# A transformer block in split float32: activations as the stationary operand, and a DMA that makes every fourth low half

## The chip, the cores and the metric

The kernel runs on one core of a Trainium2 chip. The number that counts is the device time of one execution in microseconds (us). The core's engines work side by side: TensorE (PE in the profile, its weight loads PEld), VectorE (DVE), ScalarE (ACT), GpSimd (POOL), and SyncE (SP), which here only issues transfers. They wait for each other through semaphores; 16 DMA engines carry the transfers.

## The reference

One layer of a speech-encoder block on x of 256 tokens by 2048 channels, all float32 (cut to what matters; the biases, the convolution and the scan are left out):

```python
def rms_norm(x, w):
    return x * lax.rsqrt(jnp.mean(x * x, axis=-1, keepdims=True) + NORM_EPS) * w

def swiglu(h, w_gate, w_up, w_down):            # D_FF = 5504
    return (jax.nn.silu(h @ w_gate) * (h @ w_up)) @ w_down

x = x + 0.5 * swiglu(rms_norm(x, n1), ...)      # first half-step
proj = rms_norm(x, mix_norm) @ w_in             # gdn q k v z a b | att q k v | two gates
o_gdn = gdn_branch(...)                         # gated delta rule, 8 heads of 128, chunks of 64
o_att = chunk_attention_branch(...)             # 8 heads of 128, band of 576 keys
merged = (jax.nn.sigmoid(gate_gdn) * (o_gdn @ w_branch_gdn)
          + jax.nn.sigmoid(gate_att) * (o_att @ w_branch_att))
x = x + merged @ w_out
x = x + 0.5 * swiglu(rms_norm(x, n2), ...)      # second half-step
```

Some 400 MB of weights are read once. Each product has 256 rows.

## The kernel before, in words

**Split operands.** Each float32 operand of a large product is an exact pair of float32r halves, hi + lo, and a product is hi·hi + hi·lo + lo·hi. Activations (`xr`, `hid`, `ob`, `oa`, `mg`) lie with channels on partitions, hi and lo side by side, 2 x 256 columns to a channel tile of 128.

**Pieces of weights.** `plan` lists all weights in the order of use, cut into pieces of at most 1024 columns (128 partitions x 1024, 512 KB). `prepare` takes the next piece: SP loads it to `raw` (L194), ACT casts it to `wh` (L197), DVE writes `wl` = `raw` - `wh` (L198). The pools of `raw`, `wh` and `wl` have four buffers each. `take_weights` hands the oldest piece to a product and first calls `prepare` until four pieces are on their way (AHEAD = 4); so the instructions that prepare a piece are put on their engines' queues about three pieces before PE uses it. Every engine runs its own queue in order. A cast waits until PE has done with the piece that held its `wh` buffer before.

**The large products** (`gemm_steps`, L224): a 128 x 128 weight tile is the stationary operand. One matmul takes `wh` with the 512 columns hi | lo of the activations, a second `wl` with the 256 columns hi. That makes 5536 pairs: 4128 in the two feed-forward steps (`pg`, `pu`, `pd`) and 1408 in the mixing part (`pc`, `pwb`, `pgt`, `pwa`, `pwo`); the last output tile uses another form (43 more matmuls). The result has channels on partitions, as the next product wants it. `gather` (L268, L270) joins the two halves of a result, and the factor of the norm, `rb`, the same on all partitions, is multiplied on afterwards. POOL computes the squares for the norms of the later steps.

**The attention projections and z** (`pav`, `paq`, `pak`, `pz`; `gemm_n_steps`, L258 to L260) already have activations stationary: 128 tokens x 128 channels, and the weights move, 352 or 512 columns at a time, three matmuls to a token tile.

**Order.** The program order is the order of the Python code. In the attention and delta-rule stages `weave` puts the small products of the core computation between the pieces of a large product.

Of the kernel before, what the change touches and what calls it, by code (L numbers as in the profile page):

```python
# [23 lines left out]
H = 8  # L24
# [10 lines left out]
def block_kernel(ctx: ExitStack, tc: tile.TileContext, a: dict, out: bass.AP):  # L35
    """Activations are kept transposed (channels on partitions, tokens free), each float32
    matmul operand as an exact pair of float32r halves hi + lo; a product is hi*hi + hi*lo + lo*hi."""
# [23 lines left out]
    # ---------------------------------------------------------------- residual stream  # L61
# [5 lines left out]
    x_blk = [heap([P, 8, T], F32, f"x{b}") for b in range(2)]  # L67

    def x(k):
        return x_blk[k // 8][:, k % 8, :]  # L70

    def load_x(k, n):
        nc.sync.dma_start(x_blk[k // 8][:, k % 8 : k % 8 + n, :], a["x"][:, k : k + n, :])
# [9 lines left out]
    # ---------------------------------------------------------------- helpers  # L83
    def rsqrt(dst, v, n, nm):
        """dst = v ** -0.5 for a small tile of positive v, with a Newton step."""
        s = tp.tile([P, T], F32, name=f"rs_s{nm}", tag="su", bufs=4)[:, :n]
        r = tp.tile([P, T], F32, name=f"rs_r{nm}", tag="su", bufs=4)[:, :n]
# [5 lines left out]
        nc.vector.tensor_mul(dst, r, s)  # L93

    class Xr:
        """x * norm weight as hi | lo, four channel tiles to a block; sums of squares aside."""

        def __init__(self, nm, wi):
            self.nm, self.wi = nm, wi
            self.blk = []  # L100
            self.acc = sp.tile([P, T], F32, name=f"ssq{nm}", tag="ssq", bufs=1)

        def add(self, k):
            if k % 4 == 0:
                self.blk.append(heap([P, 4, 2, T], F32R, f"xr{self.nm}_{k}"))
            b = self.blk[-1][:, k % 4]
            w = vcol(V_N[self.wi] + k)
            nc.scalar.activation(b[:, 0, :], x(k), AF.Copy, scale=w)
            nc.vector.scalar_tensor_tensor(  # L109
                b[:, 1, :], x(k), w, f32(b[:, 0, :]), op0=ALU.mult, op1=ALU.subtract  # L110
            )

        def square(self, k, act=False):
            if act:
                sq = tp.tile([P, T], F32, name=f"sq{self.nm}_{k}", tag="sq") if k else self.acc
                nc.scalar.activation(sq, x(k), AF.Square)
                if k:
                    nc.vector.tensor_add(self.acc, self.acc, sq)
            elif k == 0:
                nc.gpsimd.tensor_mul(self.acc, x(k), x(k))  # L120
            else:
                sq = tp.tile([P, T], F32, name=f"sq{self.nm}_{k}", tag="sq")
                nc.gpsimd.tensor_mul(sq, x(k), x(k))
                nc.gpsimd.tensor_add(self.acc, self.acc, sq)

        def finish(self):
            """rb: 1 / rms for every token, the same on all partitions."""
            ps = acc_bank(f"nps{self.nm}")
            nc.tensor.matmul(ps[:, 0:T], ones, self.acc, start=True, stop=True)
            v = tp.tile([P, T], F32, name=f"nv{self.nm}", tag="su", bufs=4)  # L130
            nc.vector.tensor_scalar(v, ps[:, 0:T], 1.0 / D, EPS, op0=ALU.mult, op1=ALU.add)
            self.rb = sp.tile([P, T], F32, name=f"rb{self.nm}", tag="rb", bufs=2)
            rsqrt(self.rb, v, T, f"n{self.nm}")

        def by_token(self):
            """rn: the same with tokens on partitions, a column a tile."""
            ps = core_bank(f"nbs{self.nm}")
            self.rn = sp.tile([P, 2], F32, name=f"rn{self.nm}", tag="rn")
            for t in range(2):
                nc.tensor.transpose(ps[:, t * P : (t + 1) * P], self.rb[:, t * P : (t + 1) * P], ident)  # L140
                nc.vector.tensor_copy(self.rn[:, t : t + 1], ps[:, t * P : t * P + 1])
# [4 lines left out]
    # every weight of the block, in the order of use, in pieces of at most 1024 columns  # L146
    def pieces(src, width, per):
        for o in range(0, width, per):
            yield src[:, o : min(o + per, width)]

    def t_pieces(srcs, kt):
        for src in srcs:
            yield from pieces(src, kt * P, 1024)

    def n_pieces(src, n):
        yield from pieces(src, KD * n, 1024 // n * n)

    def plan():
        for f in "12":
            tiles = [a[w + f][c] for c in range(KF) for w in ("wg", "wu")]  # L160
            for o in range(0, KD * P, 512):
                yield from (t[:, o : o + 512] for t in tiles[:4])
            yield from t_pieces(tiles[4:], KD)
            yield from t_pieces((a["wd" + f][d] for d in range(KD)), KF)
            if f == "2":
                return
            c0 = 0
            for n in ZG:
                yield from n_pieces(a["wv"][:, c0 * KD : (c0 + n) * KD], n)
                c0 += n  # L170
            for g in range(4):
                yield from n_pieces(a["wa"][g], 512)
            yield from t_pieces((a["wc"][c] for c in range(24)), KD)
            yield from t_pieces((a["wbr"][KD + d] for d in range(KD)), H)
            yield from t_pieces((a["wgt"][KD + d] for d in range(KD)), KD)
            for g in (4, 5):
                yield from n_pieces(a["wa"][g], 512)
            yield from t_pieces((a["wgt"][d] for d in range(KD)), KD)
            yield from t_pieces((a["wbr"][d] for d in range(KD)), H)
            for o in (0, 1024):  # L180
                yield from (a["wo"][d][:, o : o + 1024] for d in range(2))
            yield from t_pieces((a["wo"][d] for d in range(2, KD)), KD)
# [4 lines left out]
    def prepare():  # L187
        """Load the next piece of weights and split it."""
        i, src = next(weights, (None, None))
        if src is None:  # L190
            return
        n = src.shape[1]
        raw = wp.tile([P, 1024], F32, tag="raw", name=f"raw{i}", bufs=4)
        nc.sync.dma_start(raw[:, :n], src)  # L194
        wh = wp.tile([P, 1024], F32R, tag="wh", name=f"wh{i}")
        wl = wp.tile([P, 1024], F32R, tag="wl", name=f"wl{i}")
        nc.scalar.copy(wh[:, :n], raw[:, :n])  # L197
        nc.vector.tensor_sub(wl[:, :n], raw[:, :n], f32(wh[:, :n]))  # L198
        ready.append((wh, wl, n))

    def take_weights(n):
        for _ in range(AHEAD - len(ready)):
            prepare()
        wh, wl, m = ready.popleft()
        assert m == n
# [6 lines left out]
    def weave(core, fill):  # L212
        """Emit core, and between its steps as many pieces of fill as each step asks for."""
# [4 lines left out]
    def gemm_t(ps, kt, mov, fold=False):  # L218
        run(gemm_steps(ps, kt, mov, 8, fold))

    def gemm_steps(ps, kt, mov, per=8, fold=False):
        """ps[:, 0:256] + ps[:, 256:512] = (weights [kt*128, 128]).T @ activations, channels on partitions
        (all in the first half if fold)."""
        mm = lambda dst, w, m, st, en: nc.tensor.matmul(dst, w, m, start=st, stop=en, skip_group_check=True)  # L224
        for k0 in range(0, kt, per):
            c = min(per, kt - k0)
            wh, wl = take_weights(c * P)
            for j in range(c):
                k = k0 + j
                mv = mov(k)  # L230
                wj = slice(j * P, (j + 1) * P)
                if fold:
                    mm(ps[:, 0:T], wh[:, wj], mv[:, 0, :], k == 0, False)
                    mm(ps[:, 0:T], wh[:, wj], mv[:, 1, :], False, False)
                else:
                    mm(ps, wh[:, wj], mv.rearrange("p a t -> p (a t)"), k == 0, False)
                mm(ps[:, 0:T], wl[:, wj], mv[:, 0, :], False, k == kt - 1)
            if k0 + c < kt:
                yield

    def gemm_n(pss, kt, mov, n):
        run(gemm_n_steps(pss, kt, mov, n))

    def gemm_n_steps(pss, kt, mov, n):
        """pss[t] = activations (tokens of tile t on partitions) @ weights [kt*128, n]."""
        per = 1024 // n
        k = 0
        for o in range(0, kt, per):
            c = min(per, kt - o)
            wh, wl = take_weights(c * n)  # L250
            for j in range(c):
                mv = mov(k)
# [724 lines left out]
```

## Time and profile before

| what | value |
|---|---|
| median of 3 runs | 2174.81 us (2174.78 to 2176.48) |
| profiled execution: span from first to last instruction | 2173.8 us |
| what lies around the span: median less span | 1.0 us |
| instructions | 31985 |
| busy: PE / DVE / ACT / POOL | 2161.7 / 1406.2 / 1088.1 / 91.3 us |
| share of 16 DMA engines taken by the load queue | 56.7%, 403.58 MB |
| granted TensorE clock | 1.000 |

A group row of the profile names the line, the engine, the operation, the result and operand tiles by their names in the code, the shape and the count, then the busy time in us, the mean of one in ns, and the idle time of the engine just before them with what ended it. A matmul row of the timeline gives start and duration; matmuls overlap, so the price of one is the distance between two starts.

### The profile page before, as it was taken

Reading aid. Unit: us, or ns where it says so; the run is one execution under the profiler, and the core shown is the slowest. Engines: PE = TensorE matmul, PEld = TensorE weight load, DVE = VectorE, ACT = ScalarE, POOL = GpSimd, SP = SyncE. Lnnn points to the kernel's source line nnn. Section 1 sums busy time; section 2 is a strip of 40 time slices with the busy share of each in tenths; the row PEclk is TensorE's granted clock in tenths of the full one; section 3 lists DMA queues with packets and bytes.
Section 4 is the critical chain, followed back from the end, with each engine's and each line's share of the span. In section 5 each row is a group of like instructions: output and inputs, shape, how many; then the busy total and the mean of one; then the engine's idle time right before and its main releaser. Section 6 shows DMA issues by size and latency. Waiting matters only on the chain.

```text
span 2173.8 us, 31985 instructions
## 1 busy us (share of the span) xinstructions
PE 2161.7 (99%) x12434; PEld 1897.1 (87%) x12434; DVE 1406.2 (65%) x2034; ACT 1088.1 (50%) x1598; POOL 91.3 (4%) x99
## 2 busy tenths in 40 slices
PE   8999999999999999999999999999999999999999
PEld 7888888888888988888888888888888888888888
DVE  7766666665555554888995658767666666655444
ACT  7544444444444444576654645545444444444343
POOL 0000000000111000210000000220000000000000
PEclk9999999999999999999999999999999999999999
DMA  7555555556566665555454555546555555566664
GB/s 241 197 191 190 189 193 188 190 188 187 182 197 189 184 199 191 190 173 170 167 184 136 165 185 188 187 154 218 193 187 191 190 189 192 190 189 191 202 202 134
DMA packets 118985, 405.62 MB, mean 187 GB/s; under 512 B 13345, under 2 KB 19761, under 8 KB 118577
## 3 DMA queue, kind: packets, MB, share of 16 engines
q1 hardware_dynamic: 118832, 403.58, 56.7%
q8 instruction: 97, 1.59, 0.3%
q14 instruction: 56, 0.45, 0.1%
HBM read 401.43 MB, written 2.11 MB: 186 GB/s over the span
## 4 chain that ended last, share of the span: by engine, by line
PE 94%; DVE 3%; DMA 1%; ACT 1%; issue 1%; SPq 0%; POOL 0%; DVEq 0%; ACTq 0%
PE pd L224 22%; PE pu L224 22%; PE pg L224 21%; PE pgt L224 6%; PE pc L224 5%; PE pwo L224 4%; PE pwa L224 2%; PE pwb L224 2%; DVE wl L198 1%; PE pav L258 1%; PE pav L260 1%; PE pav L259 1%; PE pz L258 1%; PE pz L260 1%; PE pz L259 1%; PE paq L260 1%
## 5 line engine op out<-in xcount | busy, mean ns | idle before, releaser
L198 DVE TENSOR_TENSOR wl<-raw,wh 128x1024 fp32r<-128x1024 f32 (+3 forms) x798 | 938.4, 1180 | 690.7 <-ACT wh L197 689.7
L197 ACT CAST wh<-raw 128x1024 fp32r<-128x1024 f32 (+3 forms) x798 | 800.8, 1005 | 976.2 <-issue 569.7
L224 PE MATMUL pg<-xr,wh 128*128 128x512 f32 x1376 | 483.8, 394 | 6.0 <-DVE xr L109 5.9
L224 PE MATMUL pu<-xr,wh 128*128 128x512 f32 x1376 | 483.3, 393 | 0.0
L224 PE MATMUL pd<-hid,wh 128*128 128x512 f32 (+1 forms) x1419 | 477.7, 386 | 0.0
L224 PE MATMUL pg<-xr,wl 128*128 128x256 f32 x1376 | 384.4, 279 | 1.2 <-DVE wl L198 1.2
L224 PE MATMUL pu<-xr,wl 128*128 128x256 f32 x1376 | 384.0, 279 | 0.5 <-DVE wl L198 0.5
L224 PE MATMUL pd<-hid,wl 128*128 128x256 f32 x1376 | 383.3, 279 | 0.0
L224 PEld LDWEIGHTS pg<-xr,wh 128*128 128x128 f32 x1376 | 258.4, 188 | 65.0 <-ACT wh L197 6.1
L224 PEld LDWEIGHTS pd<-hid,wh 128*128 128x128 f32 x1419 | 263.0, 188 | 56.4
L224 PEld LDWEIGHTS pu<-xr,wh 128*128 128x128 f32 x1376 | 258.3, 188 | 58.5
L224 PEld LDWEIGHTS pg<-xr,wl 128*128 128x128 f32 x1376 | 259.9, 189 | 2.4 <-DVE wl L198 2.2
L224 PEld LDWEIGHTS pu<-xr,wl 128*128 128x128 f32 x1376 | 259.8, 189 | 0.9 <-DVE wl L198 0.8
L224 PEld LDWEIGHTS pd<-hid,wl 128*128 128x128 f32 x1376 | 259.3, 188 | 0.0
L224 PE MATMUL pgt<-xr,wh 128*128 128x512 f32 x512 | 181.2, 398 | 0.0
L224 PE MATMUL pgt<-xr,wl 128*128 128x256 f32 x512 | 143.2, 280 | 0.8 <-DVE wl L198 0.8
L224 PE MATMUL pc<-xr,wh 128*128 128x512 f32 x384 | 136.6, 399 | 0.0
L224 PEld LDWEIGHTS pgt<-xr,wh 128*128 128x128 f32 x512 | 96.1, 188 | 22.6
L224 PE MATMUL pc<-xr,wl 128*128 128x256 f32 x384 | 107.4, 280 | 0.0
L224 PEld LDWEIGHTS pgt<-xr,wl 128*128 128x128 f32 x512 | 96.5, 189 | 1.2 <-DVE wl L198 1.2
L224 PE MATMUL pwo<-mg,wh 128*128 128x512 f32 x256 | 90.5, 399 | 0.0
L224 PEld LDWEIGHTS pc<-xr,wh 128*128 128x128 f32 x384 | 72.1, 188 | 16.2
(269 smaller groups left out, 2080.0 us busy)
## 6 DMA issues: line engine op xcount, KB each, us to landing
raw<-wg SPq DMA_DIRECT2D x164, 512.0 KB, 3.6
raw<-wu SPq DMA_DIRECT2D x164, 512.0 KB, 3.6
raw<-wd SPq DMA_DIRECT2D x160, 512.0 KB, 4.2
raw<-wgt SPq DMA_DIRECT2D x64, 512.0 KB, 4.3
raw<-wa SPq DMA_DIRECT2D x48, 512.0 KB, 3.7
raw<-wc SPq DMA_DIRECT2D x48, 512.0 KB, 3.7
raw<-wbr SPq DMA_DIRECT2D x32, 512.0 KB, 4.1
raw<-wo SPq DMA_DIRECT2D x32, 512.0 KB, 3.4
```

Source lines behind the costliest of these rows:

```text
L197: nc.scalar.copy(wh[:, :n], raw[:, :n])
L198: nc.vector.tensor_sub(wl[:, :n], raw[:, :n], f32(wh[:, :n]))
L224: mm = lambda dst, w, m, st, en: nc.tensor.matmul(dst, w, m, start=st, stop=en, skip_group_check=True)
L258: nc.tensor.matmul(pss[t][:, :n], hi, whj, start=st, stop=False)
L259: nc.tensor.matmul(pss[t][:, :n], hi, wlj, start=False, stop=False)
L260: nc.tensor.matmul(pss[t][:, :n], lo, whj, start=False, stop=en)
```

## The change

The large products get activations as the stationary operand, as the attention projections had: `gemm_steps` now handles both. Four weight tiles, 512 columns, move at a time; for each channel tile and each of the two token tiles there are three matmuls (L274 hi x `wh`, L275 hi x `wl`, L276 lo x `wh`). In place of the 5536 pairs stand 8016 matmuls of 512 columns and 384 of 384 columns (the last group of hidden tiles has three tiles, not four). Weight files stay as they are: a piece is now two channel tiles of four weight tiles, so its load has four runs of 1 KB on a partition instead of one of 4 KB, and the moving operand is four runs of 128 columns. There are 774 pieces instead of 798. The first 16 pieces, of gate and up in turn, are 512 KB each; before, the first 16 were of 256 KB.

Results now have tokens on partitions. They are evicted 512 columns wide, with the norm's factor `rn` as a scale per partition, and what the next product needs with channels on partitions is turned back on PE (`turn`, 128 x 128 transposes, 380 in all). The residual `xn` has tokens on partitions; the input is turned once (`stand`), the output before its stores. `after(3, ...)` puts such a turn three pieces later in the program. Squares are summed on ACT.

Every fourth piece (`i % 4 == 2`, 193 of 774) gets its low half another way: ACT writes `wl` = -`wh` (L233), and a DMA issued by POOL adds `raw` to it (L234). DVE makes the other 581.

```diff
     def prepare():
...
         raw = wp.tile([P, 1024], F32, tag="raw", name=f"raw{i}", bufs=4)
-        nc.sync.dma_start(raw[:, :n], src)
         wh = wp.tile([P, 1024], F32R, tag="wh", name=f"wh{i}")
         wl = wp.tile([P, 1024], F32R, tag="wl", name=f"wl{i}")
-        nc.scalar.copy(wh[:, :n], raw[:, :n])
-        nc.vector.tensor_sub(wl[:, :n], raw[:, :n], f32(wh[:, :n]))
-        ready.append((wh, wl, n))
+        if len(src.shape) == 3:
+            m = n * kk * P
+            nc.sync.dma_start(raw[:, :m].rearrange("p (c x) -> p c x", c=n), src)
+            cols = lambda w: [w[:, :m].rearrange("p (c k x) -> p c k x", k=kk, x=P)[:, :, j, :] for j in range(kk)]
+            n *= P
...
+        nc.scalar.copy(wh[:, :m], raw[:, :m])
+        if i % 4 == 2:
+            nc.scalar.activation(wl[:, :m], f32(wh[:, :m]), AF.Copy, scale=-1.0)
+            nc.gpsimd.dma_start(wl[:, :m], raw[:, :m], accum_op=ALU.add)
+        else:
+            nc.vector.tensor_sub(wl[:, :m], raw[:, :m], f32(wh[:, :m]))
+        ready.append((cols(wh), cols(wl), n))
...
+    def turn(src, n, name):
+        for c0 in range(0, n, 2):
+            ps = core_bank(f"{name}_{c0}")
+            m = min(2, n - c0)
+            for c in range(m):
+                for t in range(2):
+                    nc.tensor.transpose(
+                        ps[:, c * T + t * P : c * T + (t + 1) * P], src(t)[:, (c0 + c) * P : (c0 + c + 1) * P], ident
+                    )
+            yield c0, m, ps[:, : m * T].rearrange("p (c t) -> p c t", c=m)
...
     def ffn(...):
...
+        for i, (c, m) in enumerate(FG):                       # groups of four hidden tiles
...
+                nc.scalar.activation(gs[t][:, :n], pg[t][:, :n], AF.Silu, scale=xr.rn[:, t : t + 1])
...
+                nc.vector.scalar_tensor_tensor(
+                    us[t][:, :n], pu[t][:, :n], xr.rn[:, t : t + 1], gs[t][:, :n], op0=ALU.mult, op1=ALU.mult
+                )
...
+            after(3, lambda c=c, m=m, us=us: hidden(c, m, us))
+        for d in range(4):
...
+                nc.vector.scalar_tensor_tensor(xn[t][:, cs], pd[t], 0.5, xn[t][:, cs], op0=ALU.mult, op1=ALU.add)
+            if nxt:
+                nxt.square(d)
+                after(3, lambda d=d: nxt.turn(d))
+            elif d < 3:
+                after(3, lambda d=d: store(d))
+            else:
+                store(d)
```

Three places show how the instructions move. The first is PE in the first feed-forward step, where one product ends and the next begins (`pg1_17`, `pu1_17`: gate and up product of hidden tile 17; `pg1_200` and `pg1_201`: gate product of the group of hidden tiles 20 to 23 for token tile 0 and 1; the number behind wh and wl is that of the piece). Before:

```order
L224 MATMUL pg1_17_2030<-xr1_12_255,wh77_1973 128x512
L224 MATMUL pg1_17_2030<-xr1_12_255,wl77_1974 128x256
L224 MATMUL pu1_17_2075<-xr1_0_108,wh78_1995 128x512 [waits Activation_49]
L224 MATMUL pu1_17_2075<-xr1_0_108,wl78_1996 128x256 [waits DVE_49]
L224 MATMUL pu1_17_2075<-xr1_0_108,wh78_1995 128x512
```

Now, with the first matmuls of piece 86, an add piece:

```order
L274 MATMUL pg1_200_1814<-wh86_1887,xr1_12_345 128x512 [waits Activation_49]
L275 MATMUL pg1_200_1814<-wl86_1888,xr1_12_345 128x512 [waits DMASW5_49]
L276 MATMUL pg1_200_1814<-wh86_1887,xr1_12_345 128x512
L274 MATMUL pg1_201_1815<-wh86_1887,xr1_12_345 128x512
L275 MATMUL pg1_201_1815<-wl86_1888,xr1_12_345 128x512
L276 MATMUL pg1_201_1815<-wh86_1887,xr1_12_345 128x512
```

Two matmuls on a weight tile became six on four tiles, and the second matmul of an add piece waits for a transfer of POOL's queue (DMASW) where it waited for DVE.

The second is ACT in the first step. Before:

```order
L197 CAST wh43_1094<-raw43_1092 128x1024 [waits DMAHW3_49,PE_49,Activation_49]
L268 COPY lou1_7_1083<-pu1_7_1032 128x256 [waits PE_49]
L197 CAST wh44_1116<-raw44_1114 128x1024 [waits DMAHW4_49,PE_49,Activation_49]
L274 CAST hid1_4_764<-suu1_7_1085 128x256 [waits DVE_49]
L197 CAST wh45_1139<-raw45_1137 128x1024 [waits DMAHW5_49,PE_49,Activation_49]
```

Now (`g1_40`, `g1_41`: the eviction of a gate product, L315):

```order
L231 CAST wh26_684<-raw26_683 128x1024 [waits DMAHW5_49,PE_49,Activation_49]
L233 ACTIVATE wl26_685<-wh26_684 128x1024 [waits DMASW5_49,Activation_49]
L315 ACTIVATE g1_40_702<-pg1_40_538,rn1_90 128x512 [waits PE_49]
L315 ACTIVATE g1_41_703<-pg1_41_539,rn1_90 128x512 [waits PE_49]
L231 CAST wh27_709<-raw27_708 128x1024 [waits DMAHW6_49,DVE_49]
L231 CAST wh28_727<-raw28_726 128x1024 [waits DMAHW7_49,DVE_49,PE_49]
```

Between the casts stood a small eviction after each piece; now there is none for several pieces, then two wide ones, and a negation follows every fourth cast.

The third is SP's queue of loads. Before:

```order
L194 DMA raw31_780<-wu1 128x1024 [waits DMAHW3_49,DVE_49]
L194 DMA raw32_802<-wg1 128x1024 [waits DMAHW4_49,DVE_49]
L194 DMA raw33_825<-wg1 128x1024 [waits DMAHW5_49,DVE_49]
L194 DMA raw34_847<-wu1 128x1024 [waits DMAHW6_49,DVE_49]
L194 DMA raw35_884<-wu1 128x1024 [waits DMAHW7_49,DVE_49]
```

Now:

```order
L224 DMA raw31_781<-wu1 128x4x256 [waits DMAHW5_49,DMASW6_49]
L224 DMA raw32_799<-wg1 128x4x256 [waits DMAHW7_49,DVE_49]
L224 DMA raw33_817<-wg1 128x4x256 [waits DMAHW0_49,DVE_49]
L224 DMA raw34_835<-wg1 128x4x256 [waits DMAHW2_49,DVE_49]
L224 DMA raw35_861<-wg1 128x4x256 [waits DMAHW1_49,DMASW7_49]
```

Every load waited for a subtraction to free its buffer; now every fourth waits for an add, the load of piece 31 for that of piece 26 and the load of piece 35 for that of piece 30, and the loads behind it stand in the queue.

More of the change, by code (lines that the diff above doesn't have):

```diff
@@ L126, in finish @@
-        def finish(self):
[L128 to L141, printed above, removed]
+            nc.scalar.activation(b[:, 0, :], src, AF.Copy, scale=w)
@@ L216, in weave, with gemm, gemm_steps @@
                 next(fill, None)
[L218 to L229, printed above, removed]
[L230 to L253 removed]
+    def gemm(pss, kt, mov, n):
+        run(gemm_steps(pss, kt, mov, n))
+    def gemm_steps(pss, kt, mov, n):
+        k = 0
+        while k < kt:
+            wh, wl = take_weights(n)
+            for whj, wlj in zip(wh, wl):
+                mv = mov(k)
                 for t in range(2):
```

427 lines of the change are left out of this document (225 added, 202 removed).

## The prediction

> **What bounds the kernel now.** I read the page's busy times and its chain of waits first.
>
> ```profile
> PE 2161.7 (99%) x12434; PEld 1897.1 (87%) x12434; DVE 1406.2 (65%) x2034; ACT 1088.1 (50%) x1598; POOL 91.3 (4%) x99
> ...
> q1 hardware_dynamic: 118832, 403.58, 56.7%
> ...
> PE 94%; DVE 3%; DMA 1%; ACT 1%; issue 1%; SPq 0%; POOL 0%; DVEq 0%; ACTq 0%
> ```
>
> TensorE (PE) is busy for 99% of the span and holds 94% of the chain. VectorE (DVE), which the change relieves, is at 65%. So a change counts where it alters the time that PE needs for a piece of weights, or where it makes a piece late. The waits show how the pieces flow today.
>
> ```profile
> DVE wl L198 <- ACT wh L197: 689.7, 626, 3.9
> ...
> ACT wh L197 <- PE pd L224: 246.0, 139, 2.3
> ...
> SPq L194 <- DVE wl L198: 1009.0, 429, 6.3
> ```
>
> VectorE waits for the cast of ScalarE (ACT), the cast waits for PE to give a buffer back, and the load queue waits for VectorE: everything ahead of PE runs early and is held back by PE. Taking subtractions off VectorE therefore buys nothing by itself. What it costs is the question.
>
> **Matmuls.** The change replaces 5536 pairs of matmuls (512 and 256 columns wide) by 8016 matmuls of 512 columns and 384 of 384. The price of a pair comes from a long window of a feed-forward (FFN) step (columns: time, busy us and count of PE, of its weight loads, of DVE, ACT, POOL, clock, DMA share, GB/s) and from the chain's longest pieces.
>
> ```profile
> 100.00:500.00 400.00, 400.00 (x2310) 349.81 (x2309) 257.93 (x359) 192.21 (x288) 0.00 (x0) 1.00 0.56 189
> ```
> ```profile
> 490.08 238.51 PE pd L224 x1376
> 1238.66 79.14 PE pgt L224 x448
> ...
> 1363.03 90.45 PE pwo L224 x512
> ```
>
> 400/1155 = 0.3463 us a pair in the FFN (the first down projection agrees: 238.51/688 = 0.3467) and 90.45/256 = 0.3533 in the mixing part. 4128 FFN pairs cost 1429.5, 1408 mixing pairs 497.4: 1927 us. The new form already runs in the attention's key projection (`pak`):
>
> ```profile
> 819.83 0.39 PE L258 MATMUL pak<-wh,xr 128*128 128x512 f32 x1
> ...
> 826.18 0.39 PE L259 MATMUL pak<-wl,xr 128*128 128x512 f32 x1
> ```
>
> 28 starts lie between these rows: 6.35/28 = 0.2268 us a matmul. 8016 of them are 1818; 384 narrower ones at 0.2268 x 384/512 = 0.170 are 65; together 1883. **The term is 1883 - 1927 = -44.** Nothing in the trace has a moving operand in four runs of 128 columns, as the new pieces have; the value taken is that of one run.
>
> **Transposes.** 380 transposes of 128x128 are new: 172 for the hidden values, 64 and 48 for the block's input to a norm and for the convolution, 32 each at the start, for the merge and for the stores. Before, four of them stand in a stream of pairs:
>
> ```profile
> 926.80 0.40 PE L224 MATMUL pc<-xr,wh 128*128 128x512 f32 x1
> 927.04 0.28 PE L224 MATMUL pc<-xr,wl 128*128 128x256 f32 x1
> 927.15 0.60 PE L398 MATMUL atrk<-cst,att_k 128*128 128x128 f32 x4
> 927.51 0.47 PE L224 MATMUL pc<-xr,wh 128*128 128x512 f32 x1
> 927.83 0.28 PE L224 MATMUL pc<-xr,wl 128*128 128x256 f32 x1
> ```
>
> From 927.15 to 927.51 are 0.36 us, and the next matmul holds its follower for 0.32 where 0.24 is usual: 0.44 for four, 0.11 each, **+42 us**. The low bound, without the second part, is 0.09 and +34. They are queued three pieces after their inputs, some 8 us, so PE should not wait for those. The products that made the norm's sums go: six `nps` of 0.38 at most, **-2**. PE's own balance is thus -4; -12 with cheap transposes, +7 if the 2112 mixing matmuls run 5 ns slower than `pak` (+11).
>
> **The added DMA.** Every fourth piece, 193 of them (call one i), gets its low half in three steps: ScalarE casts, ScalarE negates, and a DMA from POOL's queue adds the raw weights. Its cast needs the buffer that piece i-4 held, free when PE ends i-4. PE then has three pieces to work on, 3 x 12 x 0.2268 = 8.16 us, and 0.23 more for the first matmul of i, which reads the high half. Two of the three steps are in the trace:
>
> ```profile
> L198 DVE TENSOR_TENSOR wl<-raw,wh 128x1024 fp32r<-128x1024 f32 x712 | 877.0, 1236 | 641.5 <-ACT wh L197 640.7
> L197 ACT CAST wh<-raw 128x1024 fp32r<-128x1024 f32 x712 | 746.7, 1050 | 886.8 <-issue 543.4 <-PE pd L224 213.7 <-PE pak L260 22.2
> ...
> L374 ACT ACTIVATE asqk<-att_k 128x1024 f32<-128x1024 f32 x2 | 2.1, 1060 | 0.0
> ```
>
> Cast 1.05, negation 1.06 (the squares of the same shape), 0.15 for handing on: the DMA may take 8.39 - 2.26 = **6.1 us**, call it A, from issue to landing. Below that nothing waits; above, each such cycle of four pieces makes PE idle for A - 6.1. I take 150 of the 193 to be exposed, as in the gated-delta and attention stages (about 40) PE has products of their own between the pieces. Before the change this place held a subtraction of 1.24 us, whose slack was about 6 us.
>
> A is not in the trace. The nearest rows (KB each, median us to landing):
>
> ```profile
> raw<-wg SPq DMA_DIRECT2D x164, 512.0 KB, 3.6
> ...
> raw<-wd SPq DMA_DIRECT2D x160, 512.0 KB, 4.2
> ...
> raw<-wd SPq DMA_DIRECT2D x32, 192.0 KB, 2.4
> ...
> att_bias<-bias SPq DMA_DIRECT2D x1, 1024.0 KB, 6.1
> gdn_Gb<-gdn_G SPq DMA_DIRECT2D x1, 1024.0 KB, 8.0
> ```
>
> An add writes 512 KB, low bound 3.6. But it reads both operands, 1 MB: the line through 192 KB (2.4) and 512 KB (3.6) gives 5.5 at 1 MB, the bias load 6.1, the high bound is 8.0. **I take 5.7**, between the first two, since no row shows an add. That is below 6.1 by little, so the full pieces just escape. The Trainium skill, "DMA: Bandwidth & Descriptors", section on the anatomy of one DMA by the gpsimd path, gives such a transfer 2.0 us plus its bytes at 436 GB/s: an estimate of 4.4 us for 1 MB read. No row of before shows a large DMA on that queue; by it neither the short pieces below nor much of the start would wait, and the sum would be near 2177.
>
> The short pieces don't escape. In the value projection (`pav`) a piece has 12 matmuls of 0.16:
>
> ```profile
> 757.47 0.32 PE L259 MATMUL pav<-wl,xr 128*128 128x352 f32 x1
> 757.63 0.32 PE L260 MATMUL pav<-wh,xr 128*128 128x352 f32 x1
> ```
>
> There and in the narrow last hidden group the three pieces ahead last 5.8 to 6.1 us and steps and A shrink less: 12 adds late by about 0.2. In the down projections one half piece lies in each group of 22; where it is among the three ahead, A may be 4.8, so 0.9 late about six times. **+8** in all.
>
> The load queue: the load of piece i+5 waits for add i (the raw buffer), and all later loads stand behind it on SP. 2.26 + 5.7 for the add and 3.6 to 4.2 for the load end 12.2 us after PE ended i-4, and that load's cast cannot start before PE ended i+1, 13.6 after it: hidden, with 1.4 to spare.
>
> **Start and end.** Before, PE starts here:
>
> ```profile
> 5.70 0.80 PE L224 MATMUL pg<-xr,wh 128*128 128x512 f32 x1 [5.70 <-DVE xr L109]
> ```
> ```profile
> 0.00:50.00 50.00, 42.36 (x217) 35.19 (x218) 35.57 (x65) 35.07 (x67) 0.20 (x4) 1.00 0.76 251
> ```
>
> Of the first 50 us PE is idle for 7.6. The first pieces are now 512 KB, not 256: 1.0 us more of loading at this window's 251 GB/s, and a cast and a subtraction that are longer by half of 1.05 and of 1.24: 2.1 later. Piece 2 is already an add piece: 1.9 MB stand ahead of its 0.5 MB in the queue, so at 251 GB/s it lands at about 10; cast and negation end near 12.5, the add near 18, while PE, two pieces of 2.72 after 7.8, wants it at 13.3: about 5 late. Less the 1.9 that PE idles in the same stretch today, and with 1 for crowded loads after it, **+6** (bounds +2 with A at 3.6, +9 at 8.0). At the end stood one eviction:
>
> ```profile
> 2170.64 0.42 DVE L320 SCALAR_TENSOR_TENSOR x<-pd,x 128x256 f32<-128x256 f32 x1 [8.80 <-PE pd L224]
> ```
>
> Now two evictions twice as wide, eight transposes and a copy come before the last store: 0.8 + 0.9 + 0.6 less 0.4, **+2**.
>
> What costs nothing: the 32 wider evictions and per-token scales on ScalarE and VectorE are hidden behind eight pieces of PE work; the squares move from POOL to ScalarE, which is half idle; if that cover went, ScalarE's 1.06 per negation (205 us in all) would show.
>
> **The sum**: 2173.8 of span - 44 + 42 - 2 + 8 + 6 + 2 = 2185.8, and the 1.0 by which the median of the runs lies above the span: **2187 us**. About 0.2% (4.3 us) is what a measurement of this kernel can tell from no change, so 2170.5 to 2179.2 is no change.
>
> **Rivals.** *The add is slower than the lead* (slower). Place: the second matmul of every fourth piece waits for `wl`; price: 150 x (A - 6.1); it decides from A = 6.1. For it: 5.7 is close, POOL writes these descriptors in software, the 1 MB rows reach 8.0, and the DMA share of 56.7% rises by what 193 adds read, 202 MB: 202/403.58 x 56.7 = 28 points, to 85% before the shorter runs (1 KB instead of 4) of the loads; the start shows what crowding is like:
>
> ```profile
> 19.00:22.00 3.00, 3.00 (x19) 2.63 (x18) 1.97 (x4) 1.45 (x4) 0.00 (x0) 1.00 0.94 290
> ```
>
> 290 GB/s at 94%, while the new demand is 2.1 MB of loads and 1.05 MB of adds in 10.9 us, 289 GB/s. Against it: the add starts while the next loads have mostly landed. A = 7 gives 2187 + 135 = 2322, A = 8 gives 2472. One way to it has its own number: if POOL's issue waits for one running subtraction (1.24, the row above), A is 6.9 and the time 2307. The Trainium skill, "SBUF — State Buffer", section on the two separate sides, says that a VectorE instruction in a two-port mode keeps POOL from writing descriptors; no row of before tests it, as POOL issues no loads there.
>
> *The short add* (faster): A near 3.6 and transposes at 0.09. The +8 goes, the start shrinks to +2, the balance of PE is -12: 2174.8 - 12 + 2 + 2 = 2167. For it: the engine that is 99% busy gets the cheaper form, which is measured in this very kernel. Against it: the adds read twice what the 3.6 row reads.
>
> *Runs of 128 columns stream slower* (slower): no row either way. 4 ns on each of 8400 matmuls, the size by which `pgt` differs from the FFN's pairs (79.14/224 = 0.3533), are +34: 2221.
>
> *The change does not relieve anything*: VectorE falls from 65% to about 45% busy without effect on the end. That holds in all cases above, and is no case of its own.
>
> **Chances.** Forecast, 2174 to 2203: 0.44, of which 0.15 lies within the 0.2%. Slow add, 2203 to 2470: 0.21. Short add, 2160 to 2172: 0.27, nearly all faster. Slower streaming, 2203 to 2240: 0.08. So faster 0.27, no change 0.16, slower 0.57. The likeliest case's own range is 2174 to 2203; the range for 8 in 10 goes from 2162, leaving little of the short add out, to 2330 (A = 7.05), leaving 0.1 above.
>
> **What would show it.** In the new trace: PE's step in `pg`, `pu`, `pd` at 0.227 (else the streaming rival); four transposes at 0.36 to 0.44; PE's idle time ended by the add (`wl`) near zero in the steady FFN windows and the DMA row `wl<-raw` at 5 to 6 us (6.9 or more: slow add; under 4.5: short add); loads at 3.6 to 4.5, DMA share near 0.85; DVE near 1000 us busy; the first matmul near 7 and a stall of about 5 at piece 2. The forecast is wrong above all if A is more than 0.4 off upward.

## The result, and the profile after

The changed kernel takes **2205.76 us** (median of 4 runs, 2204.72 to 2209.35) against 2175.11 on the same chip: ratio 1.0126, 95% interval 1.0093 to 1.0159. (The ratios here and below are estimates with their intervals and not the quotients of the medians; here the quotient is 1.0141. Each quotient lies inside its interval.) It is slower by 30.7 us, where 12 were forecast (2187). The direction and the range for 8 in 10 (2162 to 2330) held; the likeliest case's own range, 2174 to 2203, was passed by 3 us. The profiled execution has a span of 2204.9 us.

The page of the changed kernel, in the lines that answer to those shown of before: busy times, DMA queues, chain, DMA issues.

```profile
PE 2172.8 (99%) x10091; PEld 1815.7 (82%) x10091; DVE 944.5 (43%) x1160; ACT 1216.9 (55%) x1412; POOL 175.3 (8%) x206
...
q1 hardware_dynamic: 380896, 403.58, 55.8%
q0 software_dynamic: 27792, 99.49, 25.8%
...
PE 89%; DMA 6%; ACT 2%; DVE 2%; issue 1%; SPq 0%; ACTq 0%
...
wl<-raw POOLq DMA_DIRECT2D x180, 512.0 KB, 4.9
raw<-wd SPq DMA_DIRECT2D x168, 512.0 KB, 4.6
raw<-wg SPq DMA_DIRECT2D x160, 512.0 KB, 4.6
```

VectorE is relieved (944 us, forecast about 1000), the engines of DMA are 82% taken (forecast 85%), and DMA is on the chain for 6% where it held 1%. An add takes 4.9 us in the median, less than the 5.7 that I had taken, and yet TensorE waits for it in places. TensorE's waits, longest groups (line, waited for: us in all, times, longest):

```profile
PE pg L274 <- ACT wh L231: 7.4, 1, 7.4
PE pgt L275 <- DMA wl<-raw: 5.5, 3, 2.1
PE pd L275 <- DMA wl<-raw: 3.7, 5, 1.2
PE pg L274 <- ACT g L315: 2.9, 1, 2.9
PE pg L275 <- DMA wl<-raw: 2.5, 1, 2.5
PE pav L275 <- DMA wl<-raw: 2.0, 2, 1.3
```

Four more groups bring the waits for `wl<-raw` to 16.6 us in 17 waits. They stand where they were expected (`pav`, the start) and where they were not: in the gates (`pgt`) and the down projections (`pd`). One of the latter in the timeline of TensorE:

```profile
682.18 0.39 PE L274 MATMUL pd<-wh,hid 128*128 128x512 f32 x1
683.77 0.50 PE L275 MATMUL pd<-wl,hid 128*128 128x512 f32 x1 [1.20 <-DMA wl<-raw]
```

The distance of the starts is 1.59 where 0.23 is usual: such a wait costs a little more than the idle time named in its bracket (1.36 against 1.20). Counted in this way, by starts, the late adds cost 22 us in all. The row of 2.9 us, where `pg` waits for ScalarE's `g`, was in nobody's sum.

### The profile page after: what moved, and what is told of

Same layout as the page of the kernel before. It is cut to its first block, busy times and chain, and to the rows that moved or that the text cites. A ratio compares the mean times of both kernels' runs of the same rounds, so it can differ in the third digit from the quotient of the medians.

```text
span 2204.9 us, 26549 instructions
## 1 busy us (share of the span) xinstructions
PE 2172.8 (99%) x10091; PEld 1815.7 (82%) x10091; DVE 944.5 (43%) x1160; ACT 1216.9 (55%) x1412; POOL 175.3 (8%) x206
## 3 DMA queue, kind: packets, MB, share of 16 engines
q1 hardware_dynamic: 380896, 403.58, 55.8%
q0 software_dynamic: 27792, 99.49, 25.8%
## 4 chain that ended last, share of the span: by engine, by line
PE 89%; DMA 6%; ACT 2%; DVE 2%; issue 1%; SPq 0%; ACTq 0%
PE pg L275 7%; PE pg L276 7%; PE pg L274 7%; PE pd L275 7%; PE pu L275 7%; PE pu L276 7%; PE pd L276 7%; PE pu L274 7%; PE pd L274 7%; DMA wl<-raw 5%; PE pgt L275 2%; PE pgt L276 2%; PE pgt L274 2%; PE pc L275 2%; PE pc L276 2%; PE pc L274 2%
## 5 line engine op out<-in xcount | busy, mean ns | idle before, releaser
L231 ACT CAST wh<-raw 128x1024 fp32r<-128x1024 f32 (+2 forms) x774 | 799.6, 1034 | 914.0 <-PE pd L276 229.0
L236 DVE TENSOR_TENSOR wl<-raw,wh 128x1024 fp32r<-128x1024 f32 (+4 forms) x581 | 695.6, 1198 | 1107.1 <-ACT wh L231 1104.0
L234 POOL DMA_DIRECT2D wl<-raw x193 | 166.6, 863 | 2001.4 <-ACT wl L233 1738.8
L274 PE MATMUL pg<-wh,xr 128*128 128x512 f32 (+1 forms) x704 | 274.1, 390 | 10.3 <-ACT wh L231 7.4
L275 PE MATMUL pg<-wl,xr 128*128 128x512 f32 (+1 forms) x704 | 272.5, 387 | 2.6 <-DMA wl<-raw 2.5
L275 PE MATMUL pd<-wl,hid 128*128 128x512 f32 x688 | 268.8, 391 | 3.8 <-DMA wl<-raw 3.7
L275 PE MATMUL pu<-wl,xr 128*128 128x512 f32 (+1 forms) x704 | 271.6, 386 | 0.7 <-DMA wl<-raw 0.4
L276 PE MATMUL pg<-wh,xr 128*128 128x512 f32 (+1 forms) x704 | 272.2, 387 | 0.0
L276 PE MATMUL pu<-wh,xr 128*128 128x512 f32 (+1 forms) x704 | 270.7, 384 | 0.0
L274 PE MATMUL pu<-wh,xr 128*128 128x512 f32 (+1 forms) x704 | 270.5, 384 | 0.0
L274 PE MATMUL pd<-wh,hid 128*128 128x512 f32 x688 | 268.5, 390 | 0.0
L276 PE MATMUL pd<-wh,hid 128*128 128x512 f32 x688 | 267.8, 389 | 0.0
L233 ACT ACTIVATE wl<-wh 128x1024 fp32r<-128x1024 f32 (+2 forms) x193 | 202.2, 1047 | 5.5
L274 PEld LDWEIGHTS pg<-wh,xr 128*128 128x128 f32 x704 | 132.9, 189 | 35.1 <-ACT wh L231 7.4
L275 PEld LDWEIGHTS pg<-wl,xr 128*128 128x128 f32 x704 | 133.2, 189 | 28.6 <-DMA wl<-raw 3.2
L275 PEld LDWEIGHTS pd<-wl,hid 128*128 128x128 f32 x688 | 129.1, 188 | 33.5 <-DMA wl<-raw 7.2
L275 PEld LDWEIGHTS pu<-wl,xr 128*128 128x128 f32 x704 | 132.4, 188 | 28.6 <-DMA wl<-raw 3.1
L276 PEld LDWEIGHTS pg<-wh,xr 128*128 128x128 f32 x704 | 133.1, 189 | 25.3
L274 PEld LDWEIGHTS pu<-wh,xr 128*128 128x128 f32 x704 | 132.3, 188 | 25.1
L276 PEld LDWEIGHTS pu<-wh,xr 128*128 128x128 f32 x704 | 132.4, 188 | 24.9
L276 PEld LDWEIGHTS pd<-wh,hid 128*128 128x128 f32 x688 | 129.2, 188 | 26.7
L274 PEld LDWEIGHTS pd<-wh,hid 128*128 128x128 f32 x688 | 129.1, 188 | 26.6
```

The lines of the kernel that those rows point to most:

```text
L231: nc.scalar.copy(wh[:, :m], raw[:, :m])
L233: nc.scalar.activation(wl[:, :m], f32(wh[:, :m]), AF.Copy, scale=-1.0)
L234: nc.gpsimd.dma_start(wl[:, :m], raw[:, :m], accum_op=ALU.add)
L236: nc.vector.tensor_sub(wl[:, :m], raw[:, :m], f32(wh[:, :m]))
L274: nc.tensor.matmul(dst, hi, whj, start=st, stop=False)
L275: nc.tensor.matmul(dst, hi, wlj, start=False, stop=False)
```

## The experiments

Each run's ratio is to the kernel before on its own chip; these medians of before were 2175 to 2177 us. Differences between two of these runs are taken from their medians.

**Without the adds.** Every piece is subtracted on VectorE:

```diff
-        if i % 4 == 2:
+        if False:
```

> The changed kernel without the adds: VectorE subtracts every piece, nothing else differs. Theory 'short lead' (an add piece has three pieces of lead, and the chain cast, negation, hand-over, DMA sometimes needs more): the 18.5 us in which TensorE waited for an add and some 4.5 us of slow steps behind those waits go, 2204.9 - 23 = about 2182, and no wait of TensorE for a low half above 0.3 us is left. Rival 'stationarity itself is dear' (the transposes and the lost overlap cost what was lost, the adds only stand where TensorE would wait anyway): above 2195. In both the 4.5 us at the end of the first group (61 us) stay.

Measured: 2179.99 us, ratio 1.0004 (0.9988 to 1.0021). The adds cost 2205.8 - 2180.0 = **25.8 us**, and the new matmul layout with all its transposes can hardly be told from the old (by the medians it takes 3.5 us more). Two waits of TensorE for a low half are left, 0.7 and 0.5 us, where none above 0.3 had been expected; both are for a subtraction in the gates.

**The gap at the end of the first group.** This and the next edit are made on the version without adds. First the squares of the first norm were spread over the group:

```diff
                 stand((s - 3) // 2, t)
+            xr1.square((s - 3) // 2)
         if s == 7:
...
-            for g in range(4):
-                xr1.square(g)
+            xr1.square(3)
```

> As the first of these runs (no adds), and the squares of the first norm are spread over the first group instead of standing together at its end. If TensorE's gap at 61 us (3.05 us, then seven slow steps of 0.43 us) comes from the four result banks that wait for the norm's factor, it goes: 4 to 5 us below the first run, about 2177. If it comes from the loads of that stretch, no change.

Measured: 2180.15 us, ratio 1.0015 (1.0004 to 1.0027): no gain over 2179.99, and the gap stayed at 3.3 us by the starts. The squares were not what lasts. ScalarE in that run shows what does (start, duration):

```profile
54.58 1.05 ACT L231 CAST wh<-raw 128x1024 fp32r<-128x1024 f32 x1
55.66 1.28 ACT L87 ACT_TABLE_LOAD   x1
56.95 0.20 ACT L87 ACTIVATE rs_sn<-nv 128x2 f32<-128x2 f32 x1
57.30 1.04 ACT L231 CAST wh<-raw 128x1024 fp32r<-128x1024 f32 x1
58.36 1.28 ACT L315 ACT_TABLE_LOAD   x1
59.66 1.26 ACT L315 ACTIVATE g<-pg,rn 128x512 f32<-128x512 f32 x2
```

TensorE has ended the group at 57.3. The four result banks are full, gate and up products together, and the first is read by the SiLU at 59.66, behind a square root, two table loads of 1.28 us and two casts. So the norm's factor was finished before the last two pieces instead of after them:

```diff
-            if i == 0:
+            if i == 0 and not feed:
                 xr.finish()
...
-        if s > 2 and s % 2:
-            for t in range(2):
-                stand((s - 3) // 2, t)
+        if 3 <= s <= 6:
+            for t in range(2):
+                stand(s - 3, t)
+            xr1.square(s - 3)
         if s == 7:
...
+            xr1.finish()
```

> No adds, and the input is turned two steps earlier and the norm's factor of the first step is finished before the last two pieces of the first group, not after them. If the gap at 57 us (3.3 us, then eight slow steps of 0.43 instead of 0.227) is the wait of the result banks for the chain square root, two table loads on ScalarE and SiLU, it shrinks to below 1 us and the slow steps go with it: 4 to 5 us below the run without adds, 2175. If the banks wait for something else, no change: 2180.

Measured: **2174.57 us**, ratio 0.9981 (0.9967 to 0.9995). The gap is gone, 5.4 us with its slow steps, and this version without adds is the fastest of all, ahead of the kernel before by 0.2% in the ratio and 0.1% in the medians, which is about what can be told from no change.

**What a transpose costs.** On that version, each transpose of the hidden values is done twice:

```diff
-                for t in range(2):
+                for t in (0, 0, 1, 1) if name.startswith("ht") else range(2):
```

> As the run without adds and with the early norm factor (2174.6), and each transpose of the hidden values done twice into the same place: 172 more. If transposes lie fully on TensorE's path, 172 x 0.098 (16.9 us for 172 in the trace) = 17 us more, 2191. If they fill gaps, no change.

Measured: 2192.98 us, ratio 1.0066 (1.0040 to 1.0091): 18.4 us for 172, 0.107 each: these lie fully on TensorE's path. At the same price, which was measured for the hidden values alone, all 380 are 41 us.

**Is it the short runs of the loads?** The weights were laid out so that a load is one run of 4 KB on a partition:

```diff
-            yield src[c0 : c0 + nt, :, k * P : e * P].rearrange("c p x -> p c x"), nt, e - k
+            o = c0 * kt * P + nt * k * P
+            yield src[:, o : o + nt * (e - k) * P], nt * P, e - k
...                                  # and the layout of the weight files
```

> The changed kernel with the weights laid out so that every load is one run of 4 KB on a partition, and the 512 moving columns lie side by side; the adds stay. 'Short lead': the loads become little shorter, the add not at all, so 2205 less at most 5. Rival 'crowding by the short runs of 1 KB': the loads land in 3.6 to 4.2 us as before the change, the adds in under 4.8, and most of the 23 us of late adds go: about 2185.

Measured: 2208.32 us, ratio 1.0145 (1.0131 to 1.0159); adds 4.8, loads 4.1 to 4.4 us where the changed kernel has 4.5 to 4.6. No gain: neither the runs of 1 KB nor moving operands in four runs of 128 columns cost anything that shows in the time.

**More lead, first try.** The negation is taken straight from the raw weights, ahead of the cast:

```diff
-        nc.scalar.copy(wh[:, :m], raw[:, :m])
         if i % 4 == 2:
-            nc.scalar.activation(wl[:, :m], f32(wh[:, :m]), AF.Copy, scale=-1.0)
+            nc.scalar.activation(wl[:, :m], raw[:, :m], AF.Copy, scale=-1.0)
             nc.gpsimd.dma_start(wl[:, :m], raw[:, :m], accum_op=ALU.add)
+        nc.scalar.copy(wh[:, :m], raw[:, :m])
```

> The changed kernel with the adds, but ScalarE writes the negated high half straight from the raw weights and only then casts: the add can be issued one cast (1.05 us) earlier, with the same traffic. 'Short lead': the time that an add may take rises from 5.7 to 6.8 us, most late adds go (about 5 us of waiting left, after late loads), 2204.9 - 16 = about 2189. Rival 'crowding' (adds are late because the loads and adds share the DMA engines at 85%): the same bytes in the same time, so within 5 us of 2205.

Measured: 2240.35 us, ratio 1.0292 (1.0258 to 1.0325). Both theories failed on the sign. The edit moved one thing unasked, which the order of the built program and the trace show: the load of piece i+4, itself an add piece, now waits for add i (that of piece 306 is issued at 849.68, just after add 302 has landed at 849.63), where in the changed kernel it was that of piece i+5. That made a new theory, and two runs with five raw buffers; the room comes from two scratch tiles that have two buffers instead of three. The second run has the negation first as well.

```diff
-        raw = wp.tile([P, 1024], F32, tag="raw", name=f"raw{i}", bufs=4)
+        raw = wp.tile([P, 1024], F32, tag="raw", name=f"raw{i}", bufs=5)
```

> The changed kernel with five raw buffers instead of four (room from two scratch tiles that have two buffers instead of three). The load that waits for add i is now that of piece i+6, not i+5. 'Short lead': the lead of the add itself is set by the buffers of the high and low halves, unchanged, so 2205 less the few microseconds of late loads: 2198 to 2206. Rival 'load queue' (loads that stand behind the wait for an add make the later casts late): most of the 23 us go: 2185.

> Five raw buffers, and ScalarE negates before it casts. In the earlier run with the negation first and four buffers, the load of piece i+4 (itself an add piece) waited for add i, and the time was 2240; with five it is piece i+5 again, as in the changed kernel. If that rotation was what cost 35 us, it goes, and the lead won (1.05 us an add) shows: 2185 to 2195. If negating first is itself slow (ScalarE's cast comes later for every fourth piece), it stays near 2240.

Measured: five buffers alone 2213.25 us, ratio 1.0165 (1.0152 to 1.0179); five buffers with the negation first 2277.19 us, ratio 1.0464 (1.0448 to 1.0480). The first is 7.5 us slower than the changed kernel, which neither of its theories had; whether the buffers or the scratch tiles did that is not shown. In the second the load of piece i+5 waited for add i again, as in the changed kernel, and the time was worse still: **that theory fell**. What had changed stands in the DMA issues of the two (five buffers alone; then with the negation first):

```profile
wl<-raw POOLq DMA_DIRECT2D x180, 512.0 KB, 4.9
```
```profile
wl<-raw POOLq DMA_DIRECT2D x180, 512.0 KB, 6.8
```

With the negation first the add starts a cast earlier and takes 1.9 us longer. Its start used to fall into a pause of the loads; now it starts with them. In a stretch of the steady state (the trace's issues and landings) the changed kernel issues an add at 311.89 with one load of 512 KB still under way, landing 1.5 us later, and the add takes 4.61; the negation-first kernel issues it at 309.68 behind four loads of 305.75 to 308.18, and it takes 8.15. The same can be counted over all adds of the five kernels so far that have every fourth add: the bytes that the load queue moved from 0.4 us after an add's issue to its landing. The medians of the adds are 4.5 to 4.9 us beside less than 0.3 MB and 5.3 to 6.2 beside 0.6 to 0.9 MB; in the negation-first kernel with five buffers 98 adds have 0.9 to 1.2 MB beside them and take 7.7. (A longer add also sees more loads for being longer, so this count alone would not show which is the cause.)

**Is it the loads?** On that slow kernel every odd piece reuses the raw buffer of the piece before it and is not loaded, so that half of the weights are left out:

```diff
+        again = i % 2 == 1 and prev[1] >= mm
+        if not again:
+            prev[:] = [wp.tile([P, 1024], F32, tag="raw", name=f"raw{i}", bufs=5), mm]
+        raw = prev[0]
...
+            if not again:
+                nc.sync.dma_start(raw[:, :m].rearrange("p (c x) -> p c x", c=n), src)
```

> As the run with five raw buffers and the negation first (2277, adds of 6.8 us in the median), but every odd piece is made from the raw buffer of the piece before it and not loaded: half of the weights are left out, all other instructions stay. 'Crowding' (an add that shares the DMA engines with loads in flight takes 6 to 8 us, one that is alone 4.8): the adds fall to 4.7 to 5.3 us, TensorE's waits for them to under 8 us, the time to 2180 to 2190. Rival 'the software queue itself is slow when it starts early': the adds stay above 6 us and the time above 2240.

Measured: 2188.94 us, ratio 1.0049 (1.0034 to 1.0065), from 2277. The adds and TensorE's waits for them:

```profile
wl<-raw POOLq DMA_DIRECT2D x180, 512.0 KB, 4.8
```
```profile
PE pg L282 <- DMA wl<-raw: 4.6, 1, 4.6
...
PE pgt L282 <- DMA wl<-raw: 0.9, 2, 0.7
```

All that is left of them, but 0.9 us, is the one at the start. **What lengthens these adds is the loads in flight beside them**, and with half of them out of the way the longer lead does its work. Whether they share the 16 engines or something behind these, the runs don't separate.

**How many adds.** Every eighth piece, and every second:

```diff
-        if i % 4 == 2:
+        if i % 8 == 2:               # the other run: if i % 2 == 0
```

> The changed kernel with an add for every eighth piece instead of every fourth. If each add costs on average the same (25.8 us for 193), 2180 + 13 = 2193. If the cost comes from the loads queueing behind the adds, which gets rarer faster than the adds do, near 2184.

> The changed kernel with an add for every second piece. At the same cost per add 2180 + 52 = 2232. If the DMA engines are the limit (55.8% for the loads and 2 x 25.8% for the adds are 107% of the span), at least 1.07 x 2205 = 2360.

Measured: every eighth 2186.15 us, ratio 1.0031 (1.0010 to 1.0051); every second 2470.07 us, ratio 1.1341 (1.1299 to 1.1383). Over the 2180.0 without adds: 6.2 us for 97, 25.8 for 193, 290 for 387, that is 0.06, 0.13 and 0.75 us an add. Every eighth lies nearer to the second theory's 2184 than to 2193, and every second above its 2360: the cost grows faster than the count. The late add at the start (2.5 us of waiting with every eighth and every fourth) is in each total, so without it the growth is steeper still. With every second piece the engines are full:

```profile
q1 hardware_dynamic: 380896, 403.58, 50.3%
q0 software_dynamic: 55728, 199.49, 45.0%
```

They add up to 95% of a span of 2460.4 us, and an add takes 6.1 in the median.

**The adds alone, in the kernel before.**

```diff
-        nc.vector.tensor_sub(wl[:, :n], raw[:, :n], f32(wh[:, :n]))
+        if i % 4 == 2:
+            nc.scalar.activation(wl[:, :n], f32(wh[:, :n]), AF.Copy, scale=-1.0)
+            nc.gpsimd.dma_start(wl[:, :n], raw[:, :n], accum_op=ALU.add)
+        else:
+            nc.vector.tensor_sub(wl[:, :n], raw[:, :n], f32(wh[:, :n]))
```

> The kernel before with weights stationary, and only the added DMA: every fourth piece negated on ScalarE and added by POOL's queue. 'Short lead': three pieces of 2.77 us leave 5.9 us for an add of about 4.9, so full pieces escape; where one of the three pieces ahead is the short end of a down projection (3 tiles, 1.04 us) the add is late by about 0.7, some 24 times; with the start: 2175 + 20 = 2195 (2185 to 2205). POOL also waits with its squares behind the adds. Rival 'relief' (VectorE with fewer subtractions makes evictions earlier): 2175 or below.

Measured: 2305.56 us, ratio 1.0584 (1.0561 to 1.0608): 130 us where 20 were expected. The place was right, the price was not:

```profile
PE pd L228 <- DMA wl<-raw: 53.5, 28, 4.3
```

In the down projections 28 adds are late, mostly by turns about 0.5 us and 3.3 to 3.6 by the starts. In the whole kernel the late adds cost 85 us by the starts. ScalarE and POOL ahead of one of the large ones (TensorE starts at 549.51 and next at 553.26, 3.53 late):

```profile
542.91 1.05 ACT L197 CAST wh<-raw 128x1024 fp32r<-128x1024 f32 x1 [1.81 <-PE pd L228]
544.25 1.05 ACT L197 CAST wh<-raw 128x1024 fp32r<-128x1024 f32 x1 [0.29 <-DMA raw<-wd]
545.21 1.06 ACT L199 ACTIVATE wl<-wh 128x1024 fp32r<-128x1024 f32 x1
```
```profile
546.56 0.86 POOL L200 DMA_DIRECT2D wl<-raw  x1 [11.19 <-ACT dl L322]
```

The cast of the piece behind the add piece stands before the negation (1.2 us), three narrow tiles lie among the pieces ahead (1.7 us less lead), and the add of 546.56 starts together with a load and takes 6.65 instead of 4.8. Three misses of the budget come together in one place; the new layout, whose short pieces are rarer, was hurt less.

## Why the prediction was right or wrong

**Right.** TensorE's own balance: the price of the new matmuls (the distances of their starts in the changed kernel have a median of 0.227, forecast 0.2268), of a transpose (0.107, forecast 0.11), and so the sum of the two near nothing: the layout alone, with its other terms, measures 1.0004. That VectorE's relief buys nothing: it falls to 43% busy and no step shortens. That the add's chain decides, that the short pieces make it late (below), and the DMA load of 28 points for it (25.8 measured). The streaming rival, four runs of 128 columns, is ruled out by the 0.227 and by the run with one run. POOL's waiting for a running subtraction did not happen either: the issue row of the adds is flat, and in 190 of 193 the issue starts 0.29 us after the negation.

```profile
L234 POOL DMA_DIRECT2D wl<-raw x193: 862/862/1004, 14.2 to 2183.9; - x193
```

(Minimum, median and maximum in ns.) The Trainium skill, "SBUF — State Buffer", section on the two separate sides, names that lock for VectorE's two-port modes. No trace here shows it; whether the 581 subtractions run in such a mode is not shown either, so the row rules out a wait in this kernel and does not test the rule.

**Two sizes that cancelled.** I took 5.7 us for an add and allowed 6.1. The add takes 4.9, and the allowance is 5.7: the cast starts 0.24 us after TensorE has started on the next piece, and POOL issues 0.29 after the negation, where I had 0.15 for all the handing on. That the full pieces of the feed-forward steps mostly escape came true with both sizes wrong, which was luck. Between the Trainium skill's line for 1 MB (4.4, "DMA: Bandwidth & Descriptors", anatomy of one DMA by the gpsimd path) and my 5.7 the measured value lies nearer to the former.

**The step that failed** is what the term "+8 in all" leaves out: that in the gated-delta and attention stages no add is exposed, since PE has products of its own between the pieces, and that elsewhere the full pieces "just escape". By TensorE's starts the late adds cost 22 us. Of these 2.7 are the one at 17 us, for which the start's term had about 5. Some 9.5 are adds that are narrow themselves or have a short piece among the three ahead: those that the +8 was for, so its sum was near, though two of the value projection's are 0.8 and 1.5 us late where I had 0.2. About 1.4 are full pieces whose add alone was long, 5.6 to 6.1 us. The other 8.4 us, eight adds, all stand in the mixing part, seven of them between 860 and 1140 us, where the attention and gated-delta work is that I had counted as cover; and there the chain itself came late. I had let the cast start when TensorE gives the buffer back, and each step follow the last. Two of these eight chains, at the step that was late (the first is a cast, the second an issue):

```profile
1129.66 1.05 ACT L231 CAST wh<-raw 128x1024 fp32r<-128x1024 f32 x1 [2.85 <-DMA raw<-wgt]
```
```profile
1312.00 1.06 ACT L233 ACTIVATE wl<-wh 128x1024 fp32r<-128x1024 f32 x1
1315.32 0.86 POOL L234 DMA_DIRECT2D wl<-raw  x1 [11.98 <-ACT wh L231]
```

The first cast waits for its load, which waits for subtractions that VectorE does late among its own work there: 2.5 us, and TensorE waits 2.1. In the second POOL issues 2.3 us after the negation instead of 0.29; what held it is not shown, and piece 454 has the same delay in both runs with five buffers. In others ScalarE has work of these stages ahead of the chain's steps: for the add awaited at 983 us the cast ends at 971.24, and 5.6 us of attention work lie between it and the negation. This is read from the trace of the changed kernel; no run took the delays away one by one.

I also gave the add one duration. It has a spread, 3.9 to 6.2 us in the changed kernel, and a tenth of the adds exceed 5.5. I had named crowding and then put it aside, "the add starts while the next loads have mostly landed". For most adds that is so: 151 of 193 have less than 0.3 MB of loads beside them, by the count above. But it depends on the order of issue, which one cast's shift undid (2240, and 2277 with a fifth raw buffer).

**The start, +6, was too dear.** TensorE starts 1.7 us later (7.4 against 5.7), and piece 2 is 2.5 late, not 5: its add was issued at 14.2 (the row above), 1.7 after my 12.5, but TensorE also came later: its first matmuls start 0.43 us apart, and the built order runs some matmuls of the piece behind first.

**Missing from the sum**: the full banks at the end of the first group, 5.4 us, measured by taking them away. The old first group had four banks too, but its gathers needed no norm factor to empty them; the new eviction has the factor as its scale, and so the banks wait for square root and table load. I had read "hidden behind eight pieces of PE work", which fails in the one group where both products end together.

**The end, +2**, was near: last matmul at 2198.71 of 2204.9, 6.2 us from the end, against 3.6 before (2170.25 of 2173.8): +2.6.

Together: -44 + 41 - 2 for TensorE (no run measures the -2), 22 for late adds and about 3 for the slow steps behind them, 5 for the banks, some 2 for start and 3 for the end make 30; measured are 31 of span.

## What to carry to other kernels

A transfer put into a chain with a deadline has to be priced with the loads that run beside it, not by its median alone: here 4.8 us with few loads beside it, 8.2 behind four, and issuing it earlier was worse. The deadline, too, holds only where the engines of the chain have nothing else in their queues: price it by stage. A reordering or one more buffer also moves which load waits for what, so read the built order after every such edit. And where an eviction takes a late factor as its scale, ask how many result banks are free until the factor is there.

## What was not expected of the hardware

**TensorE ran at half its clock for 3.4 us after some of its waits.** Behind the three longest waits of the changed kernel after its start (2.5, 2.9 and 2.1 us), at once or some 1.4 us later, about eight matmuls start 0.43 us apart instead of 0.227. One place in the timeline, and the window behind it (time, then busy us and counts by engine, granted clock, DMA share, GB/s):

```profile
1135.08 0.39 PE L274 MATMUL pgt<-wh,xr 128*128 128x512 f32 x1
1137.58 0.78 PE L275 MATMUL pgt<-wl,xr 128*128 128x512 f32 x1 [2.11 <-DMA wl<-raw]
1138.15 0.63 PE L276 MATMUL pgt<-wh,xr 128*128 128x512 f32 x1
1138.57 0.63 PE L274 MATMUL pgt<-wh,xr 128*128 128x512 f32 x1
```
```profile
1138.00:1141.00 3.00, 3.00 (x8) 2.35 (x8) 0.16 (x1) 0.00 (x0) 0.00 (x0) 0.50 0.78 252
```

The granted clock is 0.50 there, from 1137.6 to 1141.0. The eight steps from 1137.58 on take 3.5 us where 1.8 is usual, so the wait costs another 1.7 us; one of 1.75 us that ended at 1320.97 was followed by nothing of the kind. The length of the wait does not decide it alone. In the kernel before with the adds, this wait of 3.36 us was followed by usual steps:

```profile
553.26 0.39 PE L228 MATMUL pd<-hid,wl 128*128 128x256 f32 x1 [3.36 <-DMA wl<-raw]
553.48 0.39 PE L228 MATMUL pd<-hid,wh 128*128 128x512 f32 x1
553.71 0.28 PE L228 MATMUL pd<-hid,wl 128*128 128x256 f32 x1
```

So were six more of 3.1 to 3.4 us there, while one of 1.9 us, ended at 1131.74, was followed by 3.4 us at a granted clock of 0.50. The Trainium skill, "TensorE: Matmul & The Clock Gate", Part 1, states half rate after an idle window of about 3.4 us: the half rate agrees, but here idle times of 1.9 to 2.9 us were enough, and some of 3.1 to 3.4 us were not followed by it. What decides it is open.

**An add costs the DMA engines nearly twice the time of a load, byte for byte.** The adds' queue takes 25.8% for 99.49 MB written, the loads' 55.8% for 403.58: 0.26 and 0.14 points a MB, 1.9 to 1; in the run with half of the loads it is 1.6 to 1. The Trainium skill, "Collectives: The Full Stack", section on the fold count, explains a ratio of 1.93 between a copying and an adding collective by the two sources that an add in DMA reads. That the same holds for these adds is likely, as they read two operands, but no run here shows it.
